# Small matmuls of a head pair in turns over the two row halves, outputs of four chunks by kind

## The chip, the cores and the metric

The kernel runs on one core of one Trainium2 chip. The metric is the device time of one execution in microseconds, less is better; the figure for a kernel is the median of its timed runs.

## The reference

One layer of a hybrid decoder on a sequence of 1024 tokens with 2048 channels, all in float32. The input is RMS-normalised and multiplied by one wide matrix; the columns go to four mixers and a gate. The mixers are RWKV-7 (8 heads of 64 channels, a state of 64x64 per head that is carried from token to token by a delta rule), windowed attention (window 128, 8 query heads over 2 key heads, with sinks and a linear position bias), causal pooling, and a spatial gating unit. Their outputs are multiplied by SiLU of the gate, go through an output projection, are normalised and added to the input:

```python
h = rms_norm(x, pre_w)
za, zb, zc, zd, gate = jnp.split(h @ w_in, SPLITS, axis=-1)
ya = rwkv7_mixer(token_shift(za, mu), ...)
yb = swa_sink_attention(zb, sinks)
yc = pool_mixer(zc, pool_w, pool_scale)
yd = spatial_gating(zd, sgu_norm_w, sgu_w, sgu_b)
y = jnp.concatenate([ya, yb, yc, yd], axis=-1) * jax.nn.silu(gate)
return x + rms_norm(y @ w_out, post_w)
```

## The kernel before

The sequence is taken in two halves of 512 tokens. Channels lie on the partitions. The input projection goes in tiles of 128 columns (`proj`, L260): for each of 16 tiles of the contraction there are three products of 128x128 by 128x512 (L273, L274, L275), because weights and input are split into a high and a low part; ScalarE makes the high part of the weights (L162) and VectorE the low part (L163). The output projection (L769 to L771) has the same form.

The mixers are generators. `mixers` (L866) emits one projection per turn and then lets each mixer take a small step (`yield` ends a step), so that a mixer's small instructions stand between projections. RWKV works on pairs of heads: channels 0 to 63 of a tile are one head, 64 to 127 the other, and `H[0]`, `H[1]` are these two halves of the partitions. A matmul that contracts over one half uses one row half of the PE array. Per pair and half sequence there are 8 chunks of 64 tokens.

The places that the change touches:

- `rwkv_prep`, L395 to L404: scores of each chunk, for `q` = 0 and 1 (four chunks each) and for each head. A head's four matmuls write one PSUM tile, and VectorE evicts it in three instructions (L402 to L404).
- `rwkv_prep`, L477 to L481: transposes of a head's 8 chunks into a PSUM tile, which ScalarE copies out.
- `rwkv_chain`, `outputs` (L504): after every fourth chunk (`YB`), the outputs of these four chunks are emitted. Each chunk has two matmuls over all 128 rows (L506) and two over 64 rows (L508), which add to the same part of the tile `yp`. The chain itself (L515, L523, L528) carries the state from chunk to chunk.
- `attention`, `scores` (L587): scores of a block of 128 queries, for the two row halves `x`, and two query heads `a` in each; L595, or L598 and L599 for the first block.

PSUM tiles come from small pools: `ps_pr` has two banks (RWKV preparation and other uses), `ps_ot` two (attention and others), `ps_y` and `ps_ch` one each. A tile can be written when what read its bank before is done. For the first scores of a pair (`q` = 0) the second `ps_pr` bank holds the sums of squares `pss` (L384) until VectorE has read them (L387). For the transposes the second bank holds the product of L469 until VectorE has copied it (L471).

The order in which the program is written isn't the order in an engine's queue. The framework lays the queues out when it builds the kernel: it takes instructions by priority (earlier in the program first, the weight loads and splits ahead of them) as they become ready by its own estimate of times, so later instructions can be put before earlier ones that still wait. At run time each engine's queue is worked off with semaphores. A float32 matmul stands in the trace as two records, a transpose and a product of the two projections as one.

Of the kernel before, what the change touches and what calls it, by code (L numbers as in the profile page):

```python
"""Hybrid decoder layer (RWKV-7, windowed attention, causal pooling, spatial gating) on one core.

The sequence is taken in two halves of 512 tokens. Activations are kept with channels on the
partitions. The operands of the two large projections are split into a high part that float32r holds
exactly and the exact remainder, and three products of the parts are added up in float32.
RWKV runs in chunks of 64 tokens: each chunk's delta rule is a triangular system, whose inverse is
built from 16x16 blocks by forward substitution and then merged; the state passes from chunk to chunk.
"""
# [15 lines left out]
PSUM = bass.MemoryType.PSUM  # L24
DRAM = bass.MemoryType.DRAM

P = 128
# [5 lines left out]
HD = 64  # L33
C = 64
NC = T // C
NHP = 4
WIN = 128
# [8 lines left out]
YB = 4  # L46
# [9 lines left out]
class Layer:  # L56
    def __init__(self, tc, es, A, out):
        self.tc, self.nc, self.A, self.out = tc, tc.nc, A, out
        self.n = 0
        self.ahead = {}  # L60

        def pool(name, bufs, **kw):
            return es.enter_context(tc.tile_pool(name=name, bufs=bufs, **kw))

        self.cp = pool("const", 1)
        self.gp = pool("gen", 78)
        self.wrp = pool("wraw", 3)
        self.whp = pool("whi", 3)
        self.wlp = pool("wlo", 3)
        self.sm = pool("small", 4)  # L70
        self.fp = pool("fsub", 1)
        self.dp = pool("scratch", 2, space=DRAM)
        self.dpc = pool("blocks", 1, space=DRAM)
        self.ps_pj = pool("ps_pj", 2, space=PSUM)
        self.ps_pr = pool("ps_pr", 2, space=PSUM)
        self.ps_ch = pool("ps_ch", 1, space=PSUM)
        self.ps_y = pool("ps_y", 1, space=PSUM)
        self.ps_ot = pool("ps_ot", 2, space=PSUM)
        # the first activation loads the engine's tables while the first data is under way
        warm = self.tile(self.sm, [P, 1], "warm")  # L80
        self.nc.vector.memset(warm, 0.0)
        self.nc.scalar.activation(out=warm, in_=warm, func=AF.Square)
        self.constants()
# [57 lines left out]

# [1 line left out]
    def rsqrt(self, x, n, scale, eps):  # L143
        """1 / sqrt(x * scale + eps) for a [128, n] tile, by Newton's iteration."""
        v_ = self.nc.vector
# [18 lines left out]

# [1 line left out]
    def x_load(self, hf, k):  # L166
# [4 lines left out]
    def x_square(self, k, x, accs):  # L171
        """Adds the squares of 128 channels of each token to one of the sums."""
        nc = self.nc
# [8 lines left out]
    def x_rstd(self, hf, accs):  # L182
        """1/rms of each token of the half, along the free dim of every partition."""
        nc = self.nc
# [13 lines left out]
    def first_half(self):  # L198
        """The first half's input, whose 1/rms is applied to its projections, and that 1/rms."""
        nc = self.nc  # L200
# [50 lines left out]

# [1 line left out]
    def w_load(self, m, half):  # L253
# [23 lines left out]

# [1 line left out]
    def gate(self, j, branch):  # L279
# [7 lines left out]

# [1 line left out]
    def shift(self, pz, m, out):  # L289
# [20 lines left out]
    def head_rows(self, d, h):  # L310
        """A head's 64x64 matrices, in DRAM, as [row, chunk, column]."""
        d = d[h * NC * CSTEP:(h + 1) * NC * CSTEP].rearrange("(c r) -> c r", r=CSTEP)[:, 0:C * C]
        return d.rearrange("c (s t) -> s c t", t=C)

    def diagonal(self, d):
        """The 16x16 diagonal blocks of both heads' matrices as [block, row, column]."""
        d = d.rearrange("(i r) -> i r", r=CSTEP // 4)[:, 0:16 * C]
        return d.rearrange("i (s t) -> i s t", t=C)[:, :, 0:16]

    def rwkv_prep(self, hp):  # L320
# [37 lines left out]
        yield  # L358
        # in-context keys and keys of each chunk, (b | k) for the first head and (k | b) for the second
        bk = []  # L360
        for q in range(2):
# [3 lines left out]
            for h in range(2):  # L365
                ob, ok = slice(C * h, C * h + C), slice(C * (1 - h), C * (2 - h))
                nc.vector.tensor_tensor(out=b[H[h], :, ob], in0=v3(g1[:, qs])[H[h]], in1=v3(fa[:, qs])[H[h]], op=ALU.mult)
                nc.vector.tensor_tensor(out=b[H[h], :, ok], in0=v3(g1[:, qs])[H[h]], in1=v3(f[:, qs])[H[h]], op=ALU.mult)
        # per head: its own channels hold (a | r) of each chunk, the other half the masked key scores
        comb = [[self.g([P, 4, 2 * C]) for q in range(2)] for h in range(2)]  # L370
# [8 lines left out]
        yield  # L379
        # 1 / max(|k k_k|^2, 1e-24) with tokens of a chunk on the partitions  # L380
        pss = self.ps(self.ps_pr)
# [13 lines left out]
        for q in range(2):  # L395
            yield
            cs = slice(q * 4, q * 4 + 4)
            for h in range(2):
                p, o = self.ps(self.ps_pr, [P, 4, P]), H[1 - h]
                for c in range(4):  # L400
                    nc.tensor.matmul(p[:, c], bk[q][H[h], c, :], comb[h][q][H[h], c, :], start=True, stop=True)  # L401
                nc.vector.tensor_tensor(out=L[H[h], cs], in0=p[H[h], :, 0:C], in1=mr[H[h], cs], op=ALU.mult)  # L402
                nc.vector.tensor_tensor(out=M[H[h], cs], in0=p[H[h], :, C:2 * C], in1=mki4[H[h]], op=ALU.mult)
                nc.vector.tensor_tensor(out=comb[h][q][o], in0=p[o], in1=mk4[o], op=ALU.mult)  # L404
        yield
        # inverses of the 16x16 diagonal blocks, a block on each partition
        LB = self.tile(self.fp, [64, 16, 16], "LB")
# [19 lines left out]
        for _ in range(DMA_STEPS):  # L427
            yield
        # merges to 32, then to 64
        L32 = self.g([P, NC, C])  # L430
        nc.gpsimd.tensor_tensor(out=L32, in0=L, in1=self.m32.unsqueeze(1).to_broadcast([P, NC, C]), op=ALU.mult)

        def part(t, i):
            """The columns of the first or second 16 of every 32."""
            return t.rearrange("p c (b i u) -> p c b i u", b=2, i=2)[:, :, :, i]
# [36 lines left out]
        yield  # L472
        # tokens on the partitions: (b; k) of each head, and v beside the state
        BK = [self.g([P, NC, HD]) for h in range(2)]
        SV = [self.g([P, NC, HD]) for h in range(2)]
        UV = [self.g([P, NC, HD]) for h in range(2)]
        for h in range(2):  # L477
            p = self.ps(self.ps_pr, [P, NC, HD])
            for c in range(NC):
                nc.tensor.transpose(p[:, c], bk[c // 4][H[h], c % 4, :], self.ident[H[h], H[h]])  # L480
            nc.scalar.copy(out=BK[h], in_=p)  # L481
        p = self.ps(self.ps_pr, [P, NC, HD])
# [14 lines left out]
    def rwkv_chain(self, st):  # L497
# [5 lines left out]

        def outputs(c):  # L504
            for h in range(2):
                nc.tensor.matmul(yp[H[h], c], comb[h][c // 4][:, c % 4, C:2 * C], SV[h][:, c], start=True, stop=False)  # L506
            for h in range(2):
                nc.tensor.matmul(yp[H[h], c], M[H[h], c], UV[h][H[h], c], start=False, stop=True)  # L508

        for c in range(NC):  # L510
# [25 lines left out]
            if c % YB == YB - 1:  # L536
                for i in range(c + 1 - YB, c + 1):
                    outputs(i)
        yield
# [23 lines left out]

# [1 line left out]
    def attention(self, hf):  # L565
# [21 lines left out]
        def scores(b, g, k0):  # L587
            sc = []
            for x in range(2):
                p = self.ps(self.ps_ot, [P, 2, 2 * WIN])  # L590
                s = self.g([P, 2, 2 * WIN])
                for a in range(2):
                    qb = q[2 * g + a][H[x], b * P:(b + 1) * P]
                    if b:
                        nc.tensor.matmul(p[:, a], qb, kd[g][H[x], (b - 1) * P:(b + 1) * P], start=True, stop=True)  # L595
                        continue
                    if hf:
                        nc.tensor.matmul(p[:, a, 0:WIN], qb, self.kprev[g][H[x]], start=True, stop=True)  # L598
                    nc.tensor.matmul(p[:, a, WIN:], qb, kd[g][H[x], 0:P], start=True, stop=True)  # L599
                for a in range(2):  # L600
# [63 lines left out]

# [1 line left out]
    def pooling(self, hf):  # L666
# [36 lines left out]

# [1 line left out]
    def gating_unit(self):  # L705
# [48 lines left out]

# [1 line left out]
    def out_weights(self, cb, i, hi, lo):  # L756
        """Two 128-row tiles of a 512-column block of w_out, split."""
        with self.tc.high_priority():
# [25 lines left out]
    def out_proj(self, hf, back=None):  # L784
# [28 lines left out]
        if not last:  # L813
            for _ in back:
                pass
            return ssq
        # the last column block, one token tile after the other
        w = []
# [47 lines left out]
    def mixers(self, hf, back, start):  # L866
        """Emits the projections, and between them the mixers' work in small steps."""
        self.y, self.y_split, fed = [None] * KT, [], 1
# [126 lines left out]
```

## Time and profile before

| | |
|---|---|
| median of 3 timed runs | 1835.55 us (1832.64 to 1838.29) |
| span of the profiled execution, first to last instruction | 1831.1 us |
| between span and median | 4.45 us |
| PE busy | 1783.8 us, 97% of the span |
| VectorE busy | 986.4 us, 54% |
| ScalarE busy | 615.8 us, 34% |
| GpSimd busy | 347.2 us, 19% |
| DMA | 190 MB, mean 104 GB/s |

The profiled execution's own time is its span and what lies around it (the start and end of the program, which hold no instruction). Busy means that at least one instruction of the engine was under way. The lines of the trace are read with their tiles: `ps_pr<-g,g` is a matmul into a tile of pool `ps_pr` from two tiles of pool `g`. In "64*128 64x128" the stationary operand has 64 rows and 128 columns, and the moving one 64 rows and 128 columns.

### The profile page before, as it was taken

How to read it: one execution, taken by the hardware profiler on the slowest of the kernel's cores; microseconds unless marked ns; L12 is line 12 of the kernel's file. 1: busy time of each engine (PE TensorE's matmuls, PEld its weight loads, DVE VectorE, ACT ScalarE, POOL GpSimd, SP SyncE). 2: the span in 40 equal slices, each digit the busy share in tenths (PEclk: the TensorE clock that was granted, in tenths of full speed). 3: DMA queues.
4: the chain of work that ended last, by engine and by line, in shares of the span. 5: the costliest groups of instructions: out<-in, count | busy, mean ns of one | idle time of the engine just before them, and what ended most of it. 6: DMA issues, size and time to landing. Idle time of an engine off the chain costs nothing.

```text
span 1831.1 us, 26853 instructions
## 1 busy us (share of the span) xinstructions
PE 1783.8 (97%) x10352; PEld 1359.3 (74%) x10352; DVE 986.4 (54%) x2186; ACT 615.8 (34%) x1205; POOL 347.2 (19%) x506
## 2 busy tenths in 40 slices
PE   7999999999999999999999999999999999999997
PEld 5787677667767877788877876677777678778875
DVE  6654676476456644753346446754753564353335
ACT  6323333433333322433232333333323323242230
POOL 4111231122134311110002223311220220100002
PEclk9999999999998999999999998999999899999999
DMA  6342113123223312454333532342232132224445
GB/s 205 101 120 76 59 54 96 58 70 103 93 86 94 119 58 70 144 168 129 130 114 105 164 105 80 110 142 76 70 102 76 52 98 73 71 77 123 146 134 201
DMA packets 58144, 190.00 MB, mean 104 GB/s; under 512 B 8400, under 2 KB 8400, under 8 KB 58016
## 3 DMA queue, kind: packets, MB, share of 16 engines
q1 hardware_dynamic: 44672, 147.34, 25.1%
q0 software_dynamic: 13200, 40.91, 7.6%
q8 instruction: 81, 1.33, 0.3%
q14 instruction: 47, 0.39, 0.1%
q10 hardware_dynamic: 144, 0.03, 0.0%
HBM read 168.86 MB, written 18.87 MB: 103 GB/s over the span
## 4 chain that ended last, share of the span: by engine, by line
PE 86%; DVE 7%; issue 3%; DMA 1%; ACT 1%; POOL 0%; DVEq 0%; SPq 0%; ACTq 0%; POOLq 0%
PE ps_pj L273 18%; PE ps_pj L274 17%; PE ps_pj L275 17%; PE ps_pj L769 3%; PE ps_pj L771 3%; PE ps_pj L770 3%; PE ps_pr L769 3%; PE ps_pr L771 3%; PE ps_pr L770 3%; PE ps_pr L401 2%; PE ps_y L508 1%; DVE wl L163 1%; PE ps_ot L643 1%; PE ps_pr L442 1%; PE ps_ch L523 1%
## 5 line engine op out<-in xcount | busy, mean ns | idle before, releaser
L163 DVE TENSOR_TENSOR wl<-wr,wh 128x512 fp32r<-128x512 f32 x488 | 346.9, 712 | 512.1 <-ACT wh L162 493.7
L273 PE MATMUL ps_pj<-g,wh 128*128 128x512 f32 x1472 | 603.6, 410 | 12.2 <-ACT g L212 12.2
L275 PE MATMUL ps_pj<-g,wl 128*128 128x512 f32 x1472 | 595.0, 404 | 5.4 <-DVE wl L163 5.2
L162 ACT CAST wh<-wr 128x512 fp32r<-128x512 f32 x488 | 301.7, 620 | 877.0 <-PE ps_pj L274 624.8
L274 PE MATMUL ps_pj<-g,wh 128*128 128x512 f32 x1472 | 594.9, 404 | 0.0
L273 PEld LDWEIGHTS ps_pj<-g,wh 128*128 128x128 f32 x1472 | 281.1, 191 | 84.7 <-ACT g L212 12.2
L275 PEld LDWEIGHTS ps_pj<-g,wl 128*128 128x128 f32 x1472 | 280.6, 191 | 74.1 <-DVE wl L163 7.1
L274 PEld LDWEIGHTS ps_pj<-g,wh 128*128 128x128 f32 x1472 | 280.6, 191 | 67.2 <-issue 4.9
L518 POOL TENSOR_SCALAR SD<-g,g 64x64 f32<-64x64 f32 x128 | 63.3, 494 | 523.2 <-DVE g L531 367.1
L769 PE MATMUL ps_pj<-wh,g 128*128 128x512 f32 x224 | 88.6, 396 | 0.4 <-DVE g L879 0.2
L769 PE MATMUL ps_pr<-wh,g 128*128 128x512 f32 x224 | 88.4, 395 | 0.0
L771 PE MATMUL ps_pr<-wh,g 128*128 128x512 f32 x224 | 88.3, 394 | 0.0
L770 PE MATMUL ps_pr<-wl,g 128*128 128x512 f32 x224 | 88.2, 394 | 0.0
L770 PE MATMUL ps_pj<-wl,g 128*128 128x512 f32 x224 | 88.1, 393 | 0.0
L771 PE MATMUL ps_pj<-wh,g 128*128 128x512 f32 x224 | 88.0, 394 | 0.0
L811 POOL DMA_DIRECT2D dram_o<-g x24 | 13.0, 541 | 246.5 <-DVE g L781 243.1
L531 DVE SCALAR_TENSOR_TENSOR g<-ps_ch,g,SD 64x64 f32<-64x64 f32 x112 | 31.7, 283 | 51.2 <-PE ps_ch L528 48.8
L879 DVE TENSOR_TENSOR g<-ps_pj,g 128x512 f32<-128x512 f32 x45 | 30.9, 687 | 46.8 <-PE ps_pj L275 46.1
L417 DVE TENSOR_TENSOR ftmp<-t,LB 64x1 f32<-64x1 f32 (+14 forms) x120 | 45.3, 377 | 14.7 <-DMA LB<-dl 11.4
L769 PEld LDWEIGHTS ps_pj<-wh,g 128*128 128x128 f32 x224 | 42.1, 188 | 10.9 <-DVE g L879 0.7
L769 PEld LDWEIGHTS ps_pr<-wh,g 128*128 128x128 f32 x224 | 42.1, 188 | 10.4 <-DVE g L781 0.7
L771 PEld LDWEIGHTS ps_pj<-wh,g 128*128 128x128 f32 x224 | 42.1, 188 | 10.0
(239 smaller groups left out, 2111.9 us busy)
## 6 DMA issues: line engine op xcount, KB each, us to landing
wr<-in_w_in SPq DMA_DIRECT2D x188, 512.0 KB, 3.7
wr<-in_w_out SPq DMA_DIRECT2D x64, 512.0 KB, 3.6
g<-in_xT POOLq DMA_DIRECT2D x32, 256.0 KB, 6.0
g<-in_x POOLq DMA_DIRECT2D x32, 256.0 KB, 4.7
out_y<-g SPq DMA_DIRECT2D x32, 256.0 KB, 3.9
dram_o<-g POOLq DMA_DIRECT2D x24, 256.0 KB, 3.5
g<-dram_o POOLq DMA_DIRECT2D x24, 256.0 KB, 4.1
g<-in_xT SPq DMA_DIRECT2D x16, 256.0 KB, 5.9
```

The source lines that it names most:

```text
L162: self.nc.scalar.copy(out=hi, in_=raw)
L163: self.nc.vector.tensor_tensor(out=lo, in0=raw, in1=hi.bitcast(F32), op=ALU.subtract)
L273: nc.tensor.matmul(p, hi[:, kk], hh, start=k == 0, stop=False)
L274: nc.tensor.matmul(p, hi[:, kk], hl, start=False, stop=False)
L275: nc.tensor.matmul(p, lo[:, kk], hh, start=False, stop=k == KT - 1)
L401: nc.tensor.matmul(p[:, c], bk[q][H[h], c, :], comb[h][q][H[h], c, :], start=True, stop=True)
L417: nc.vector.tensor_tensor(out=tmp[:, 0:i, 0:i], in0=T16[:, 0:i, 0:i].rearrange("p j c -> p c j"), in1=LB[:, 0:i, i].unsqueeze(1).to_broadc ...
L518: nc.gpsimd.tensor_scalar(out=SD[H[h]], in0=SV[h][H[h], c], scalar1=E[H[h], c, C:C + 1], scalar2=None, op0=ALU.mult)
L531: nc.vector.scalar_tensor_tensor(out=SV[h][H[h], c + 1], in0=pt[H[h], 2], scalar=E[H[h], c, C:C + 1], in1=SD[H[h]], op0=ALU.mult, op1=ALU.add)
L769: nc.tensor.matmul(p, yh[:, ms], hi, start=k == 0, stop=False)
L770: nc.tensor.matmul(p, yh[:, ms], lo, start=False, stop=False)
L771: nc.tensor.matmul(p, yl[:, ms], hi, start=False, stop=k == KT - 1)
```

## The change

In the scores of RWKV, the transposes and the attention scores, the PSUM tiles of both row halves are taken before the first matmul, and the matmuls alternate between the halves instead of finishing one half first. The evictions follow as before, half by half. In `outputs` the matmuls of four chunks are grouped by kind: first the eight over 128 rows, then the eight over 64 rows. Since all chunks share one PSUM bank, only the first chunk now carries the `start` flag. No instruction is added or taken away. Comments and docstrings are blanked (not shown).

```diff
-            for h in range(2):
-                p, o = self.ps(self.ps_pr, [P, 4, P]), H[1 - h]
-                for c in range(4):
-                    nc.tensor.matmul(p[:, c], bk[q][H[h], c, :], comb[h][q][H[h], c, :], start=True, stop=True)
+            pq = [self.ps(self.ps_pr, [P, 4, P]) for h in range(2)]
+            for c in range(4):
+                for h in range(2):
+                    nc.tensor.matmul(pq[h][:, c], bk[q][H[h], c, :], comb[h][q][H[h], c, :], start=True, stop=True)
+            for h in range(2):
+                p, o = pq[h], H[1 - h]
...
+        pb = [self.ps(self.ps_pr, [P, NC, HD]) for h in range(2)]
+        for c in range(NC):
+            for h in range(2):
+                nc.tensor.transpose(pb[h][:, c], bk[c // 4][H[h], c % 4, :], self.ident[H[h], H[h]])
         for h in range(2):
-            p = self.ps(self.ps_pr, [P, NC, HD])
-            for c in range(NC):
-                nc.tensor.transpose(p[:, c], bk[c // 4][H[h], c % 4, :], self.ident[H[h], H[h]])
-            nc.scalar.copy(out=BK[h], in_=p)
+            nc.scalar.copy(out=BK[h], in_=pb[h])
...
-        def outputs(c):
-            for h in range(2):
-                nc.tensor.matmul(yp[H[h], c], comb[h][c // 4][:, c % 4, C:2 * C], SV[h][:, c], start=True, stop=False)
-            for h in range(2):
-                nc.tensor.matmul(yp[H[h], c], M[H[h], c], UV[h][H[h], c], start=False, stop=True)
+        def outputs(cs):
+            for c in cs:
+                for h in range(2):
+                    nc.tensor.matmul(yp[H[h], c], comb[h][c // 4][:, c % 4, C:2 * C], SV[h][:, c], start=c == 0,
+                                     stop=False, skip_group_check=True)
+            for c in cs:
+                for h in range(2):
+                    nc.tensor.matmul(yp[H[h], c], M[H[h], c], UV[h][H[h], c], start=False, stop=c == NC - 1,
+                                     skip_group_check=True)
...
             if c % YB == YB - 1:
-                for i in range(c + 1 - YB, c + 1):
-                    outputs(i)
+                outputs(range(c + 1 - YB, c + 1))
...
-            for x in range(2):
-                p = self.ps(self.ps_ot, [P, 2, 2 * WIN])
-                s = self.g([P, 2, 2 * WIN])
-                for a in range(2):
+            px = [self.ps(self.ps_ot, [P, 2, 2 * WIN]) for x in range(2)]
+            for a in range(2):
+                if b == 0 and hf:
+                    for x in range(2):
+                        nc.tensor.matmul(px[x][:, a, 0:WIN], q[2 * g + a][H[x], 0:P], self.kprev[g][H[x]], start=True, stop=True)
+                for x in range(2):
                     qb = q[2 * g + a][H[x], b * P:(b + 1) * P]
                     if b:
-                        nc.tensor.matmul(p[:, a], qb, kd[g][H[x], (b - 1) * P:(b + 1) * P], start=True, stop=True)
-                        continue
-                    if hf:
-                        nc.tensor.matmul(p[:, a, 0:WIN], qb, self.kprev[g][H[x]], start=True, stop=True)
-                    nc.tensor.matmul(p[:, a, WIN:], qb, kd[g][H[x], 0:P], start=True, stop=True)
+                        nc.tensor.matmul(px[x][:, a], qb, kd[g][H[x], (b - 1) * P:(b + 1) * P], start=True, stop=True)
+                    else:
+                        nc.tensor.matmul(px[x][:, a, WIN:], qb, kd[g][H[x], 0:P], start=True, stop=True)
+            for x in range(2):
+                p = px[x]
+                s = self.g([P, 2, 2 * WIN])
```

## Rows read from the trace of the kernel before

**Rows 1.** Page, part 4: chain that ended last, shares by engine.

```profile
PE 86%; DVE 7%; issue 3%; DMA 1%; ACT 1%; POOL 0%; DVEq 0%; SPq 0%; ACTq 0%; POOLq 0%
```

**Rows 2.** Groups by line on PE: busy us, mean ns of one, idle before.

```profile
L401 PE MATMUL ps_pr<-g,g 64*128 64x128 f32 x256 | 39.1, 320 | 4.3 <-DVE g L374 4.3
...
L508 PE MATMUL ps_y<-g,g 64*64 64x64 f32 x256 | 32.7, 249 | 0.0
...
L506 PE MATMUL ps_y<-g,g 128*64 128x64 f32 x256 | 26.8, 241 | 0.0
...
L595 PE MATMUL ps_ot<-g,g 64*128 64x256 f32 x96 | 20.8, 423 | 0.0
...
L480 PE MATMUL ps_pr<-shapes,g 64*128 64x64 f32 x128 | 11.8, 234 | 0.0
```

**Rows 3.** Timeline of PE, 79 to 85 us: start, length, line, count.

```profile
79.82 1.13 PE L401 MATMUL ps_pr<-g,g 64*128 64x128 f32 x8 [1.51 <-DVE g L374]
...
82.16 0.40 PE L275 MATMUL ps_pj<-g,wl 128*128 128x512 f32 x1
82.50 1.14 PE L401 MATMUL ps_pr<-g,g 64*128 64x128 f32 x8
...
84.13 0.39 PE L275 MATMUL ps_pj<-g,wl 128*128 128x512 f32 x1
84.36 0.40 PE L273 MATMUL ps_pj<-g,wh 128*128 128x512 f32 x1
```

**Rows 4.** Timeline of PE, 93 to 96 us.

```profile
93.45 1.71 PE L401 MATMUL ps_pr<-g,g 64*128 64x128 f32 x16
```

**Rows 5.** Timeline, first, second and last pass: eviction L387 and the first head's run.

```profile
82.20 0.16 DVE L387 TENSOR_SCALAR r<-ps_pr 128x8 f32<-128x8 f32 x1
...
227.47 1.16 PE L401 MATMUL ps_pr<-g,g 64*128 64x128 f32 x8
227.58 0.17 DVE L387 TENSOR_SCALAR r<-ps_pr 128x8 f32<-128x8 f32 x1 [0.36 <-PE ps_pr L384]
...
1454.45 1.82 PE L401 MATMUL ps_pr<-g,g 64*128 64x128 f32 x8 [0.63 <-DVE g L374]
...
1456.57 0.16 DVE L387 TENSOR_SCALAR r<-ps_pr 128x8 f32<-128x8 f32 x1
```

**Rows 6.** Timeline of PE, 186 to 189 us: outputs of a half head pair.

```profile
186.62 0.34 PE L515 MATMUL ps_ch<-g,g 128*64 128x64 f32 x4
...
187.00 0.33 PE L508 MATMUL ps_y<-g,g 64*64 64x64 f32 x4
187.26 0.34 PE L506 MATMUL ps_y<-g,g 128*64 128x64 f32 x4
187.53 0.33 PE L508 MATMUL ps_y<-g,g 64*64 64x64 f32 x4
...
188.06 0.66 PE L635 MATMUL ps_ot<-shapes,g 128*128 128x128 f32 x4
```

**Rows 7.** Timeline of PE: half of one score call, and a whole one.

```profile
252.69 1.13 PE L595 MATMUL ps_ot<-g,g 64*128 64x256 f32 x4
...
279.08 1.14 PE L595 MATMUL ps_ot<-g,g 64*128 64x256 f32 x8
```

**Rows 8.** Timeline, 159 to 161 us: first transposes, and evictions L471.

```profile
159.94 0.71 PE L480 MATMUL ps_pr<-shapes,g 64*128 64x64 f32 x8
160.05 0.85 DVE L471 COPY g<-ps_pr 32x256 f32<-32x256 f32 x2 [0.51 <-PE ps_pr L469]
```

**Rows 9.** Timeline of PE, 205 us: two row halves, two banks.

```profile
205.09 0.69 PE L330 MATMUL ps_pr<-g,g 64*128 64x512 f32 x1
205.10 0.69 PE L332 MATMUL ps_pr<-g,g 64*128 64x512 f32 x1
```

**Rows 10.** Spans and clocks: granted TensorE clock, mean.

```profile
core 0: 1831.1 us, clock 0.977
```

## The prediction

> **What bounds the kernel now.** I read the chain that ended last first, because it says whose time counts: PE holds 86% of it [rows 1], so a microsecond of PE time is worth about one microsecond of the end. Then the groups by line on PE. The lines that the change touches are busy for 39.1 (L401), 32.7 (L508), 26.8 (L506), 20.8 (L595) and 11.8 us (L480) [rows 2], 131 us together; more than a part of that can't be had. The timelines show how long a run of such records really takes, and what stands between two runs. The reader is to see there how much two row halves already run side by side.
>
> **What the change does to the queue.** The number of matmuls, DMAs and evictions stays the same, and so does the number of banks. Only PE's order moves, and no other queue, SP's and POOL's included, gets or loses an instruction. So each part is a question: do the records of two row halves overlap more than today?
>
> **What a run costs today.** A head's four score matmuls (eight records) take 1.13 to 1.14 us [rows 3]. Seen in the stream of projections: from the product at 82.16 to the one at 84.13 there are 1.97 us with three products and the run; a product takes 0.23 (84.13 to 84.36), so the run costs 1.97 - 0.69 = 1.28 us [rows 3].
>
> **How far the halves overlap today.** Matmuls of two row halves into two banks can start 0.01 us apart [rows 9]. And they do so without being written in turns: a run of 16 score records, first head then second, takes 1.71 us, not twice 1.13 [rows 4]; eight records of attention scores, first four of one half and then four of the other, take 1.14 us, as long as four records alone (1.13) [rows 7]. So PE looks ahead about four records: with runs of four per half the overlap is whole, with runs of eight it is half.
>
> The Trainium skill ("TensorE: Matmul & The Clock Gate", Part 3, the mechanism) says that only weight loads are pulled ahead and that matmuls are strictly first in, first out. By that rule a run that is written half by half would be serial today, and each of the 16 RWKV score groups and 12 attention calls would halve, which is the rival of full pairing below. The rows disagree: 1.71 us for 16 and 1.14 for 8 [rows 4, 7].
>
> **RWKV scores, second four chunks (`q` = 1).** Here the 16 records stand together [rows 4]; there are eight such groups (four head pairs, two halves). Written in turns they overlap whole and take as long as eight alone: 1.71 - 1.14 = 0.57 us less, 8 times: 4.5 us. Between 0 (the look-ahead doesn't change) and 4.5 I take 4.5, since in attention runs of four, and so surely runs of two, overlap whole [rows 7].
>
> **RWKV scores, first four chunks (`q` = 0).** Here the heads' runs stand apart, the first at 79.82, the second at 82.50 with projections between [rows 3]. The reason is the second bank: VectorE evicts `pss` from it at 82.20 [rows 5], and only then can the second head write. The change doesn't free that bank sooner, and the planner takes what is ready: the first head's four matmuls will go ahead as now. Upper bound: both runs in one, 1.28 us less, 8 times: 10.2 us. Lower bound: 0. I take 2.0, one microsecond for each of the two of the eight groups in which L387 falls inside the first head's run, as at 227.58 in the run from 227.47 [rows 5].
>
> **Transposes.** The first head's eight take 0.71 us from 159.94 and are done at 160.65; the second bank is evicted by L471 from 160.05 to 160.90 [rows 8]. The second head comes too late to overlap, in turns or not. Between 0 and 0.71 x 8 = 5.7 us I take 0.
>
> **Attention scores.** A call that stands together overlaps whole already [rows 7]. Others are broken up by the RWKV chain's instructions or by a bank that isn't free, and stay so. Upper bound: the 12 calls of L595 at 1.14 us each [rows 7] take 13.7 of today's 20.8 us [rows 2]: 7.1. I take 1.0.
>
> **Outputs.** After L515 of a chunk the planner puts the outputs that are ready: L506, L508, L506, L508, L506, four records each, 1.44 us from 186.62 to 188.06, L515's records included [rows 6]; there are 16 such stretches, two per pair and half. Each change between 128 rows and 64 costs: L515 with L506, eight records of one shape, take 0.38 (186.62 to 187.00), four of L506 between two changes 0.27 (187.26 to 187.53). So four more records cost 0.11, and the change 0.16. Grouped by kind there are 16 records of 128 rows (0.16 + 4 x 0.11 = 0.60) and 8 of 64 rows (0.26 from 187.00 to 187.26, and 0.11: 0.37): 0.97 instead of 1.44, 0.47 less, 16 times: 7.5 us. Lower bound 0, if L506 of the last chunk, which waits for the chain's state, were to hold back the group; I don't take it, since in the rows the planner puts ahead what is ready. The evictions of `yp` come a step later, so a projection covers an output that is put back.
>
> **Evictions.** The first head's eviction now waits for the last but one matmul of both. Paired, that is again about 1.1 us after the start [rows 3]: nothing. If the second head is late, at most the first's eviction comes that much later, and the projection that stands between two steps (48 products of 0.23 us, 11 us) covers it.
>
> **Sum.** 4.5 + 2.0 + 0 + 1.0 + 7.5 = 15.0 us. The profiled span of 1831.1 becomes 1816.1; the timed median lies 4.45 us above the span, so 1835.55 becomes **1820.5 us**.
>
> **Rivals.**
>
> *Full pairing.* If the planner, given the turns, waits for both banks with other work in between and then issues both heads together, every part gets its upper bound: 10.2 + 4.5 + 5.7 + 7.1 + 7.5 = 35.0 us, 1800.5 us. For it: projections are always there to fill in. Against it: the first head's matmuls are ready earlier and are now taken as soon as they are [rows 3]. The skill's rule on strict order would give this number too.
>
> *The second bank holds up the queue.* If the second head's first matmul stands second in PE's queue, all behind it waits: the other three matmuls of the first head, and the projections after them, until L387: 2.54 us at first (79.82 to 82.36), 0.28 at 227.47, 2.28 at last (1454.45 to 1456.73) [rows 3, 5], 15.6 us over the eight; and for the transposes until L471, 0.96 us (159.94 to 160.90) [rows 8] 8 times, 7.7. Less the gains that the pairing then brings (10.2 + 4.5 + 5.7 + 7.5 = 27.9) that leaves 4.6 us: 1831 us. The Trainium skill ("TensorEngine Tiling (Array Packing)", Restrictions and Gotchas, PSUM pressure) names this price: row tiles need banks of their own. A cousin is that the gain goes into waits on VectorE (L401 waits 4.3 us for it already [rows 2]): 1835.5. Both are no change by the measure here.
>
> *The clock.* The mean granted clock is 0.977 [rows 10]; with the two levels 2.4 and 1.2 GHz that is 4.6% of the span, 84 us, at the lower one, which costs 42 us. The last pass shows one: eight records take 1.82 us instead of 1.13, after PE had waited 0.63 us for VectorE [rows 3, 5]. These stages have small matmuls and waits. If the denser runs leave more waiting and the time at the lower level grows by 30 us, the gain is gone; from 41 us on the kernel is slower by over 0.3%; if it doubles, it is 42 - 15 = 27 us slower, 1862 us. For it: the fall lies where the change works. Against it: the same work in less time with projections moving up should rather raise PE's activity.
>
> **How the numbers follow.** The forecast 0.47 (1812 to 1828), full pairing 0.15, held queue or lost gain 0.23, the clock 0.15. Differences within 0.3%, 5.5 us, can't be told from no change. Faster: 0.47 + 0.15 = 0.62; same 0.23; slower 0.15. The range reaches from 1797 (just past full pairing) to 1840 (lost gain, and the first of the clock): it leaves out nearly all of the clock's 0.15 and a little of full pairing, under 2 in 10. The forecast's own range is 1812 to 1828: half of the sum, or the sum with the first scores (5.1 for 2.0), the transposes (2.8 for 0) and attention (3.5 for 1.0) at half their upper bounds.
>
> **What would show it.** After the change the 16-record runs of L401 last about 1.14 us, not 1.71, at all eight places of `q` = 1; for `q` = 0 two runs of eight still stand apart. After L515 there is a run of 12 L506 and one of 8 L508 records, about 0.97 us in all. L480 still stands in two runs of eight, L595's calls take 1.14 us as before. Full pairing shows as 16 L480 records in under 0.9 us. The held queue shows as idle time of PE in front of L401 and L480, released by L387 and L471. The clock shows in the mean granted clock, under 0.977. Wrong would be: runs of 16 that still take 1.7 us, or shape changes that cost nothing in the new order.

## The result, and the profile after

The changed kernel takes 1805.23 us (median of 4 runs, 1799.19 to 1812.52) against 1835.74 us for the kernel before, a ratio of 0.984 with a 95% interval of 0.9807 to 0.9872: 30.5 us less, where 15.0 were predicted, so twice the forecast. The time lies inside the range and below the 1812 to 1828 of the forecast itself.

The views of after in the order of those of before. The spans and clocks, which answer to [rows 10]:

```profile
core 0: 1806.3 us, clock 0.981
```

The chain that ended last, shares by engine, which answers to [rows 1]:

```profile
PE 83%; DVE 9%; issue 3%; DMA 3%; ACT 1%; POOL 1%; DVEq 0%; SPq 0%; POOLq 0%; ACTq 0%
```

PE is still the bound. The profiled span is 24.8 us shorter, and part of that is the clock. What the lower clock level costs a span, reckoned as the prediction did, is the span times what the mean clock lacks to one: 1831.1 x 0.023 = 42.1 us before, 1806.3 x 0.019 = 34.3 after. So 7.8 of the 24.8 us are clock, and 17.0 are work and waits. The time of every execution on record is 1.7 to 1.9 us above its own span (1808.09 and 1806.3 in the profiled one). The 4.45 us between span and median before were therefore mostly spread between executions, and the 30.5 us of the medians hold some of that spread too.

The groups by line, which answer to [rows 2] (L515 was L508, L511 was L506, L604 was L595, L482 was L480):

```profile
L401 PE MATMUL ps_pr<-g,g 64*128 64x128 f32 x256 | 32.6, 315 | 5.9 <-DVE g L374 5.9
L515 PE MATMUL ps_y<-g,g 64*64 64x64 f32 x256 | 22.0, 239 | 0.0
L604 PE MATMUL ps_ot<-g,g 64*128 64x256 f32 x96 | 20.7, 420 | 0.0
L511 PE MATMUL ps_y<-g,g 128*64 128x64 f32 x256 | 19.1, 229 | 0.1
L482 PE MATMUL ps_pr<-shapes,g 64*128 64x64 f32 x128 | 11.8, 234 | 0.0
```

The two lines of the outputs fell from 59.5 to 41.1 us busy, the scores from 39.1 to 32.6. Attention and transposes stand where they stood. The reader is to see here where to look first: the largest fall is in the outputs, not in the scores.

PE's timeline in four places: the first scores (`q` = 0) from 79 us, the second scores (`q` = 1) from 97, the transposes from 163, and one attention call at 308:

```profile
79.36 2.05 PE L401 MATMUL ps_pr<-g,g 64*128 64x128 f32 x8 [1.53 <-DVE g L374]
...
97.10 0.40 PE L275 MATMUL ps_pj<-g,wl 128*128 128x512 f32 x1
97.42 1.16 PE L401 MATMUL ps_pr<-g,g 64*128 64x128 f32 x16
98.51 0.50 PE L273 MATMUL ps_pj<-g,wh 128*128 128x512 f32 x1
...
163.40 0.71 PE L482 MATMUL ps_pr<-shapes,g 64*128 64x64 f32 x8
...
164.93 0.71 PE L482 MATMUL ps_pr<-shapes,g 64*128 64x64 f32 x8
...
308.38 1.14 PE L604 MATMUL ps_ot<-g,g 64*128 64x256 f32 x8
```

Sixteen score records last 1.16 us, where they lasted 1.71 [rows 4], as predicted. At `q` = 0 the first head's eight records go alone, as before; at one of the eight places only (1118.86 us) the heads stand together. The transposes are two runs of eight, and a whole attention call takes 1.14 us as it did [rows 7].

The outputs of one half of a head pair, which answer to [rows 6]:

```profile
190.07 0.34 PE L523 MATMUL ps_ch<-g,g 128*64 128x64 f32 x4
190.23 0.52 PE L511 MATMUL ps_y<-g,g 128*64 128x64 f32 x12
190.69 0.66 PE L645 MATMUL ps_ot<-shapes,g 128*128 128x128 f32 x4
...
194.39 0.33 PE L511 MATMUL ps_y<-g,g 128*64 128x64 f32 x2
...
195.25 0.28 PE L511 MATMUL ps_y<-g,g 128*64 128x64 f32 x2
195.46 0.50 PE L515 MATMUL ps_y<-g,g 64*64 64x64 f32 x9
...
196.78 0.33 PE L515 MATMUL ps_y<-g,g 64*64 64x64 f32 x2
```

This isn't what was predicted. The twelve records over 128 rows stand where they were expected, and with the four of L523 they take 0.62 us to the next instruction (predicted 0.60). But the eight over 64 rows don't follow. They come only behind the last chunk's four of L511, at 195.46, 4.8 us after the place where they were expected (190.69), and then mostly in one run.

### The profile page after: what moved, and what is told of

The parts are those of the page before. It is cut to its first block, busy times and chain, and to the rows that moved or that the text cites. A ratio compares the mean times of both kernels' runs of the same rounds, so it can differ in the third digit from the quotient of the medians.

```text
span 1806.3 us, 26854 instructions
## 1 busy us (share of the span) xinstructions
PE 1754.0 (97%) x10352; PEld 1344.7 (74%) x10352; DVE 988.4 (55%) x2186; ACT 614.9 (34%) x1205; POOL 347.8 (19%) x506
## 4 chain that ended last, share of the span: by engine, by line
PE 83%; DVE 9%; issue 3%; DMA 3%; ACT 1%; POOL 1%; DVEq 0%; SPq 0%; POOLq 0%; ACTq 0%
PE ps_pj L273 18%; PE ps_pj L274 17%; PE ps_pj L275 17%; PE ps_pj L779 3%; PE ps_pj L781 3%; PE ps_pj L780 3%; PE ps_pr L780 3%; PE ps_pr L781 3%; PE ps_pr L779 3%; DVE wl L163 1%; PE ps_pr L401 1%; PE ps_pr L444 1%; DVE ftmp L419 1%; PE ps_y L515 1%; PE ps_ot L653 1%
## 5 line engine op out<-in xcount | busy, mean ns | idle before, releaser
L779 PEld LDWEIGHTS ps_pr<-wh,g 128*128 128x128 f32 x224 | 42.2, 188 | 10.6 <-DVE g L791 0.8
L781 PEld LDWEIGHTS ps_pj<-wh,g 128*128 128x128 f32 x224 | 42.1, 188 | 9.8
```

Of the source, the lines that this page charges most:

```text
L779: nc.tensor.matmul(p, yh[:, ms], hi, start=k == 0, stop=False)
L781: nc.tensor.matmul(p, yl[:, ms], hi, start=False, stop=k == KT - 1)
```

## The experiments

Two measures stand in what follows. The **ratio** is to the kernel before, with its 95% interval. The **clock-free difference** is a kernel's mean span times its mean granted clock over all its runs, less the same for the kernel before (1833.4 x 0.9770 = 1791.2, 59 runs). It takes out what the prediction's reckoning gives to the clock. The other kernels have 4 to 12 runs, `runs4` one. A **run** of outputs is an unbroken series of matmuls of one of the two output lines, in the order in which PE starts them (one of a matmul's two records is counted). A **change of rows** is a place where two records that PE starts one behind the other contract over different numbers of rows (128, 64 or 32) and at least one of them is an output; it is counted over all records.

| kernel | median us | ratio | mean clock | clock-free difference, us |
|---|---|---|---|---|
| changed | 1805.23 | 0.984 (0.9807 to 0.9872) | 0.9835 | -17.2 |
| changed, timed again | 1808.81 | 0.9848 (0.9811 to 0.9885) | 0.9818 | -18.0 |
| `outputs_only` | 1811.24 | 0.9854 (0.983 to 0.9879) | 0.9812 | -16.5 |
| `scores_only` | 1836.68 | 1.0007 (0.9985 to 1.0028) | 0.9765 | 0.0 |
| `bk_att_only` | 1832.83 | 0.9971 (0.9953 to 0.9989) | 0.9775 | -1.1 |
| `three_one` | 1828.29 | 0.9967 (0.9944 to 0.9989) | 0.9786 | -3.9 |
| `late` | 1821.85 | 0.9918 (0.9886 to 0.995) | 0.9743 | -19.6 |
| `late_both` | 1816.92 | 0.9895 (0.9861 to 0.9929) | 0.9803 | -12.5 |
| `step_late` | 1801.22 | 0.9811 (0.9782 to 0.984) | 0.9804 | -26.9 |
| `all_late` | 1794.04 | 0.9775 (0.9747 to 0.9803) | 0.9815 | -31.3 |
| `all_late_plain` | 1799.56 | 0.9811 (0.9784 to 0.9837) | 0.9796 | -29.3 |
| `runs4` | 1808.81 (one run) | | 0.981 | -18.5 |

### Each part alone

Each is the kernel before with hunks of the change as they are printed in its diff above. `outputs_only` has `outputs` and its call:

```diff
-        def outputs(c):
+        def outputs(cs):
...
-                for i in range(c + 1 - YB, c + 1):
-                    outputs(i)
+                outputs(range(c + 1 - YB, c + 1))
```

`scores_only` has the turns of the RWKV scores:

```diff
+            pq = [self.ps(self.ps_pr, [P, 4, P]) for h in range(2)]
+            for c in range(4):
+                for h in range(2):
+                    nc.tensor.matmul(pq[h][:, c], bk[q][H[h], c, :], comb[h][q][H[h], c, :], start=True, stop=True)
...
```

`bk_att_only` has the turns of the transposes and of attention:

```diff
+        pb = [self.ps(self.ps_pr, [P, NC, HD]) for h in range(2)]
...
+            px = [self.ps(self.ps_ot, [P, 2, 2 * WIN]) for x in range(2)]
...
```

The changed kernel was timed again beside `three_one`, `late` and `late_both`.

> The kernel before with the outputs of four chunks grouped by kind, and nothing else changed. Theory 1 (PE's records): most of the gain is here; the two lines of the outputs take about 16 us less from start to next start, as in the changed kernel, so 1835.7 becomes about 1820, with three runs per half head pair (12 and 4 records over 128 rows, then 12 over 64 rows) where there were eleven. Theory 2 (the clock): about 12 us of the measured 30 come from fewer stretches at the lower clock, and not from these lines; then this part alone gives 16 us only if the mean granted clock stays near 0.977, and up to 25 us if it rises to 0.985.

> The kernel before with the RWKV scores alone written in turns. Theory 1: eight runs of 16 records take 1.09 us in place of 1.64 to the next start, 4.5 us less; the first four chunks still stand in two runs of eight and give nothing: about 1831. Theory 2: the clock moves by itself with any new order, so the time may lie anywhere within 10 us of 1831 and the granted clock tells where. Rival: if the second bank held up the queue, PE would idle in front of the scores and the time would be 1835 or more.

> The kernel before with the transposes and the attention scores written in turns. Theory 1: nothing moves that counts: the transposes still stand in two runs of eight of 0.64 us, whole attention calls still take 1.07 us to the next start: 1835 plus or minus 3. Theory 2: if the lower clock is set off by chance by any change of order, this kernel too leaves 1835 by more than 5 us with a clock other than 0.977.

> The changed kernel once more, for the spread of its granted clock: 1800 to 1813 us, and about 1809 us of span when brought to a mean clock of 0.98 with the slope of 16 us per 0.01 that the runs so far show. If the gain were mostly a matter of the clock, the clock would fall back to 0.976 in some of these runs and the time to 1820.

The outputs alone bring nearly the whole gain (-16.5 of about -17.5), transposes and attention together -1.1, the scores nothing where about 1831 us was expected. Yet the scores' run is shorter in `scores_only` too. PE's timeline there, in two places:

```profile
97.29 1.16 PE L401 MATMUL ps_pr<-g,g 64*128 64x128 f32 x16
...
1172.82 0.39 PE L274 MATMUL ps_pj<-g,wh 128*128 128x512 f32 x1
1174.78 0.66 PE L637 MATMUL ps_ot<-shapes,g 128*128 128x128 f32 x4 [1.56 <-ACT g L678]
```

and PE's waits by line there: total, times, longest (L401 has its 4.2 us as before, 4.3):

```profile
PE ps_ot L676 <- DVE g L604: 3.0, 3, 1.8
...
PE ps_ot L637 <- ACT g L678: 2.1, 2, 1.6
```

The same transposes in the kernel before, PE's waits:

```profile
PE ps_ot L635 <- ACT g L676: 0.4, 1, 0.4
```

Laid side by side record by record, the profiles of before and of `scores_only` differ by 4.1 us at the scores, all of it gained. Attention gives back 1.4, other small stages 2.4, the stretches with equal instructions 1.3, and stretches at the lower clock in either profile gain 0.7; the first product starts 0.9 us earlier. The spans lie 0.7 us apart (1830.4 and 1831.1). So the term was there in PE's records and not in the end. Waits for other engines explain a part of that: without the first wait of the kernel, PE is idle for 36.9 us where it was idle for 35.1, and the wait of L637 for ScalarE alone is 1.7 us longer, most of it at 1174.78. Where the other 2.3 us of the 4.1 went isn't shown: each of these places may pay for the scores, or for the planner's new order as such.

### Why the outputs brought twice the term

Theory: the matmuls that write one PSUM tile are kept in written order. All eight chunks share one tile, so behind `wide` of the fourth chunk, which waits for the chain's state, the 64-row ones of the first three are held too, and the runs become longer than predicted. `three_one` writes down the order that the prediction had assumed; everything else is as in the change.

```diff
+            def wide(cc):
+                for c in cc:
+                    for h in range(2):
+                        nc.tensor.matmul(yp[H[h], c], comb[h][c // 4][:, c % 4, C:2 * C], SV[h][:, c], start=c == 0,
+                                         stop=False, skip_group_check=True)
+
+            def half(cc):
+                for c in cc:
+                    for h in range(2):
+                        nc.tensor.matmul(yp[H[h], c], M[H[h], c], UV[h][H[h], c], start=False, stop=c == NC - 1,
+                                         skip_group_check=True)
+
+            wide(cs[0:3])
+            half(cs[0:3])
+            wide(cs[3:4])
+            half(cs[3:4])
```

> The changed kernel with the outputs in the order that the prediction expected: over 128 rows for the first three chunks, over 64 rows for these three, then both kinds for the fourth. Theory 1 (writes to one bank stay in the written order, so that the changed kernel holds the 64-row outputs back behind the fourth chunk's and so makes runs of 12 of them): this order splits them again, 8 and four times 2 records; it gives up half of the outputs' gain, 8 us slower than the changed kernel at the same clock, about 1817 of span at 0.98. Rival (only the changes of shape in the stretch behind the third chunk count): 0.97 us in that stretch as predicted, and the same time as the changed kernel.

PE's timeline in `three_one` (L531 is the chain's, L512 over 128 rows, L518 over 64):

```profile
185.57 0.34 PE L531 MATMUL ps_ch<-g,g 128*64 128x64 f32 x4
185.74 0.52 PE L512 MATMUL ps_y<-g,g 128*64 128x64 f32 x12
186.19 0.45 PE L518 MATMUL ps_y<-g,g 64*64 64x64 f32 x8
186.57 0.66 PE L653 MATMUL ps_ot<-shapes,g 128*128 128x128 f32 x4
```

Here is the predicted stretch to the letter: 12 and 8 records, 1.00 us from 185.57 to 186.57, predicted 0.97. And the kernel gains 3.9 us clock-free, not 17: at the same clock it is about 14 us slower than the changed kernel, where 8 were expected. So the stretch was priced well, and its order was the wrong one: it is the held order that brings the rest. Only the written order differs between the two kernels, so the hold by written order is shown. Nor did all of the stretch's price reach the end. PE is busy for 1770.6 of 1826.5 us here and for 1783.8 of 1831.1 before, so its idle time went from 47.3 to 55.9 us. The largest rise is at the chain, before (first) and in `three_one`:

```profile
PE ps_ch L523 <- DVE X L521: 3.4, 8, 1.4
...
PE ps_ch L539 <- DVE X L537: 6.7, 10, 1.9
```

If long runs are what counts, the outputs should be held longer still. `step_late` issues each four chunks one step later, when the fourth's state is ready; `all_late` issues all eight behind the whole chain.

```diff
         for c in range(NC):
             yield
+            if c == 4:
+                outputs(range(4))
...
-            if c % YB == YB - 1:
-                outputs(range(c + 1 - YB, c + 1))
         yield
+        outputs(range(4, NC))
```

In `all_late` the first two added lines are left out, and the last is `outputs(range(NC))`.

> The changed kernel with the outputs of four chunks emitted one step later, when the fourth chunk's state is there: 16 and 16 records in one go, 32 runs in PE's queue in place of 110. Theory 1: 78 runs fewer, up to 20 us less than the changed kernel at the same clock, 1789 of span at 0.98, and all_late no more than 5 us better than this. Rival as for all_late: 1806 or more.

> The changed kernel with the outputs of all eight chunks emitted a step after the chain, 32 records over 128 rows and then 32 over 64 rows at eight places: 16 runs in PE's queue where the changed kernel has 110 and the kernel before 180. Theory 1 (what is paid is each separate run, with a change of shape into it and out of it, about 0.26 us by the 18 us that 70 fewer runs gave): 94 runs fewer, up to 24 us less than the changed kernel at the same clock, 1785 of span at 0.98; half of it, 12 us, if the chain's steps miss the outputs as filling. Rival (the outputs were useful filling while the chain waits for VectorE): PE idles in the chain instead, and the time is 1806 or more.

PE's timeline in `step_late`:

```profile
203.44 0.69 PE L511 MATMUL ps_y<-g,g 128*64 128x64 f32 x16
204.05 0.68 PE L515 MATMUL ps_y<-g,g 64*64 64x64 f32 x16
204.66 0.34 PE L525 MATMUL ps_ch<-g,g 128*64 128x64 f32 x4
```

PE's timeline in `all_late`:

```profile
243.91 1.15 PE L511 MATMUL ps_y<-g,g 128*64 128x64 f32 x32
245.00 1.15 PE L515 MATMUL ps_y<-g,g 64*64 64x64 f32 x32
246.07 1.16 PE L401 MATMUL ps_pr<-g,g 64*128 64x128 f32 x16
```

Sixteen records of one kind hold PE for 0.61 us, thirty-two for 1.09. The second sixteen thus cost 0.48, 0.03 a record, and 0.13 us is left as the price of each change of shape; the prediction had 0.16 and 0.11 for four records from [rows 6]. The outputs' time on PE goes with the number of changes. "To the next start" is the sum over the outputs' records of the time until PE starts its next record, with time at the lower clock counted half:

| kernel | runs of outputs | changes of rows | busy us, both lines | to the next start, us | PE idle, us |
|---|---|---|---|---|---|
| before | 180 | 206 | 59.5 | 45.2 | 47.3 |
| `three_one` | 132 | 162 | 48.9 | 38.4 | 55.9 |
| changed | 110 | 112 | 41.1 | 30.5 | 52.3 |
| `step_late` | 32 | 26 | 21.9 | 19.6 | 56.6 |
| `all_late` | 16 | 10 | 18.4 | 17.3 | 53.3 |

In busy time that is between 0.22 and 0.26 us for each run fewer than before (10.6 / 48, 18.4 / 70, 37.6 / 148, 41.1 / 164). To the next start it is between 0.14 and 0.16 us for each change of rows fewer (6.8 / 44, 14.7 / 94, 25.6 / 180, 27.9 / 196), near the price of 0.13 read off two single stretches. In clock-free time a run fewer is worth 0.25, 0.18 and 0.19 us in the last three kernels and 0.08 in `three_one`; the end doesn't follow PE's records one for one, since changed overlaps and waits elsewhere count in it too. Number and place of the runs move together in these kernels, so the end's gain isn't split between fewer changes and a later place; PE's own time to the next start is what the count explains.

The expectations had up to 20 us less than the changed kernel at the same clock for `step_late`, and for `all_late` up to 24, or 12 if the chain misses the filling; about 9 and 14 came. `all_late` is the fastest kernel of the study, 1794.04 us.

Does it need the turns? `all_late_plain` is the kernel before with `all_late`'s outputs and no turns anywhere.

```diff
-            if c % YB == YB - 1:
-                for i in range(c + 1 - YB, c + 1):
-                    outputs(i)
         yield
+        outputs(range(NC))
```

> The kernel before with all_late's outputs and nothing of the turns: scores, transposes and attention as before the change. Theory 1 (the turns shorten eight runs of scores by 0.55 us, but attention then waits for VectorE by about as much): within 2 us of all_late at the same clock, 1795 to 1798 of span at 0.98. Rival (the turns' 4.4 us come through once the outputs no longer fill the waits): 4 us or more slower than all_late, 1800 or more.

It gives -29.3 against -31.3: all three sets of turns together are worth about 2.0 us there, and 0.7 to 1.5 between `outputs_only` and the changed kernel. The medians lie 5.5 us apart, but their intervals of the ratio overlap, and much of the 5.5 is the clock (0.9796 and 0.9815).

### What the turns do to PE

`runs4` writes the scores in turns of two matmuls (four records) for each head instead of one.

```diff
-            for c in range(4):
+            for c0 in (0, 2):
                 for h in range(2):
-                    nc.tensor.matmul(pq[h][:, c], bk[q][H[h], c, :], comb[h][q][H[h], c, :], start=True, stop=True)
+                    for c in (c0, c0 + 1):
+                        nc.tensor.matmul(pq[h][:, c], bk[q][H[h], c, :], comb[h][q][H[h], c, :], start=True, stop=True)
```

> The changed kernel with the RWKV scores in turns of two matmuls (four records) per head in place of one. Theory 1 (PE starts a matmul of the other row half past four waiting records): the 16 records of the second four chunks take as long as in strict turns, 1.09 us to the next start, at all eight places where they stand together. Rival (matmuls start strictly in the order of the queue): the second of each pair of runs waits for the first, 1.6 us or more.

PE's timeline in `runs4`:

```profile
97.10 1.26 PE L402 MATMUL ps_pr<-g,g 64*128 64x128 f32 x16
98.29 0.50 PE L273 MATMUL ps_pj<-g,wh 128*128 128x512 f32 x1
```

From start to next start the sixteen take 1.19 us, in strict turns 1.09 (97.42 to 98.51 above). Half by half they last 0.55 us longer than in turns (1.71 against 1.16). So runs of four overlap nearly whole and runs of eight only in part, as the prediction read from [rows 4, 7]. The starts of the single records say the same. In strict turns the sixteen start as eight pairs, at most 0.01 us apart. Half by half, in the kernel before, four start alone first, and three pairs in all are found; in fours there are seven pairs, the first of them at once. A record of the second head thus starts past three or four waiting ones of the first, and "by half" was a little too much for runs of eight. The queue itself isn't in the trace: that it held the records as written, and that PE did the pairing and not the planner, is taken for granted here. The Trainium skill ("TensorE: Matmul & The Clock Gate", Part 3) keeps matmuls in program order and lets only weight loads go ahead; by that rule the second head would start behind all eight records of the first, and eights would last nearly two times 1.13 us. The rows show 1.71, and in fours 1.26.

### Giving the second bank time

The changed kernel's first scores wait 1.53 us for VectorE and then last 2.05 us for eight records (above), where a run at the full clock lasts 1.13 [rows 3]; the granted clock is 0.50 there, 1.2 GHz:

```profile
79.40:84.20 4.80, 4.80 (x15) 3.54 (x15) 3.52 (x10) 0.63 (x1) 1.04 (x1) 0.50 0.27 94
```

The wait alone can't be the reason, since the kernel before waits as long at the same place (1.51 us [rows 3]) and has a granted clock of 1.00 from 77 to 83 us. Theory: without that wait there is no fall of the clock there, and the heads pair up as well. `late` issues the scores of `q` = 0 two steps later; `late_both` also the transposes (the last two added lines).

```diff
         for q in range(2):
             yield
+            if q == 0:
+                yield
+                yield
...
+        yield
+        yield
         BK = [self.g([P, NC, HD]) for h in range(2)]
```

> The changed kernel with the first four chunks' scores two steps later, behind the next projection. Theory 1 (the second bank, held by the sums of squares until VectorE has read them, keeps the heads apart): now both banks are free, the 16 records stand together at all eight places and take 1.09 us, so 1.28 us less each, 10 us in all, and PE no longer waits for VectorE in front of them, so that the stretches at the lower clock there (about 35 us in the changed kernel) go too, up to 17 us more: 1778 to 1797. Rival: the preparation ends a projection later and the chain's end is exposed where no projection is left: 1805 or more.

> As the last, and the transposes two steps later too. Theory 1: the 16 transposes stand together and take half the time, about 0.7 us less at eight places, 5 us under the last: 1773 to 1792. Rival: the transposes are bound by the loads of their stationary operand and pair worse (16 in 1.0 us or more), or the later chain costs what they give: the same as the last or slower.

PE's timeline and waits in `late`:

```profile
89.12 1.16 PE L404 MATMUL ps_pr<-g,g 64*128 64x128 f32 x16
90.22 0.50 PE L273 MATMUL ps_pj<-g,wh 128*128 128x512 f32 x1
```

```profile
PE ps_ot L687 <- DVE g L615: 13.2, 2, 8.4
```

PE's timeline, and its waits, in `late_both`:

```profile
178.19 0.71 PE L487 MATMUL ps_pr<-shapes,g 64*128 64x64 f32 x16
```

```profile
PE ps_pr L570 <- POOL g L563: 14.9, 4, 7.1
...
PE ps_ot L689 <- DVE g L617: 10.3, 4, 4.5
```

The pairs came in part. In `late` the wait is gone, and of the eight groups of `q` = 0 two stand as unbroken sixteens; in the other six both heads' records stand close together, but cut by other instructions. In `late_both` four of all sixteen groups are unbroken, and at all eight places sixteen transposes last 0.71 us, as long as eight. The time didn't follow (expected were 1778 to 1797 and 1773 to 1792 us). `late` is at -19.6 (the changed kernel -17.2 and -18.0), with a mean clock of 0.9743: in its profile PE is at the lower clock for 87 us, where the changed kernel has 71, for the most part at other places, so the theory that the falls vanish falls. PE waits 13.2 us at L687 for VectorE, where after had 3.0 at the same place. `late_both` is at -12.5: the lines behind the transposes come later, and PE waits for POOL 14.9 us at L570, 1.4 in the kernel before and after.

Not tried: both heads' scores in one bank.

## Why the prediction was right or wrong, point by point

- **Scores, `q` = 1 (-4.5).** The mechanism and its size are right in the records: 0.55 us at each place where the sixteen stood unbroken before. Those are six of the eight, not all; attention's records cut the other two. Over all scores PE's time falls by 4.1 us in `scores_only`. In the time it isn't there (`scores_only`, 0.0). The step that failed is the first sentence of all, that a microsecond of PE's time is worth about one of the end: 1.8 us of it are more waiting, most of it for ScalarE, and the rest stays open. With long runs of outputs part of it seems to stay (2.0 us for all the turns).
- **Scores, `q` = 0 (-2.0).** One group of eight paired, not two. Right in kind; what it is worth in the time isn't shown by itself.
- **Transposes (0) and attention (-1.0).** The runs are unchanged, as predicted, and the two edits alone give -1.1. That this is attention's 1.0 isn't shown: in the changed kernel attention's records take as long to the next start as before (27.0 and 26.8 us).
- **Outputs (-7.5).** The direction and the price of a change of shape are right, the size is off by more than two: 16.5 measured. The step that failed is "in the rows the planner puts ahead what is ready". The lower bound had named the case in which the last chunk holds back the group, as a loss. It happened, and was a gain: held records come in longer runs. The sum also priced one stretch of five runs, where a half head pair has about eleven (180 / 16), and left the others as they were. Where exactly the predicted order was written (`three_one`), PE's time in the outputs fell by 6.8 us, near the 7.5, but only 3.9 came out at the end.
- **Sum (-15.0).** 17.0 clock-free in the profiles: nearly the forecast, because the outputs' surplus stands against the scores' missing gain. That is luck: the two largest terms are each wrong at the end, in opposite directions.
- **The clock.** The prediction took the clock as it was, and as a rival only for the worse, with the remark that less waiting should rather help. It helped: 0.977 to 0.981 in the profiles, 7.8 us, and 0.9770 to 0.9835 in the mean of the runs, which is 1810 x 0.0065 = 12 us; timed again, the changed kernel had 0.9818, 9 us. That brings the time below the forecast's own range. Of the single parts only the outputs carry it (0.9812 in `outputs_only`, 0.9765 and 0.9775 in the two others), and not in every kernel that has them (0.9743 in `late`). Why a longer run of outputs leaves less time at the lower level isn't settled.
- **Rivals.** Full pairing didn't happen, though its 1800.5 us is close to the result; in `late_both`, where all transposes paired and the scores did in pieces, the later steps cost more than the pairs gave; pairing without the delay wasn't tried. The held queue didn't either: L401 waits 5.9 us, not 15.6. But its cousin, the gain that goes into waits, happened to a part of the scores' term.

## What to carry to other kernels

Count the changes of matmul shape in PE's queue, above all between numbers of rows: small matmuls into one tile took least time here in one run for each shape, and holding them until all of their inputs are there can be worth more than issuing each as soon as it is ready (1794 against 1805 us here). Turns over the row halves shorten a run that is longer than PE's look-ahead, but test whether the time saved on PE reaches the end, because here it was gone at the end, in part into waits for other engines. Where a kernel's span is part clock, compare spans at equal clock before you give a difference to an edit.

## What the runs showed that was not expected

- Sixteen small matmul records in a row hold PE for 0.61 us and thirty-two for 1.09, 0.03 us a record, with 128 rows as with 64; a change between the two shapes costs 0.13 us there, and 0.14 to 0.16 over whole kernels. Of the 45.2 us of the outputs before, 512 records at 0.03 are 15 us, so the two kinds in four-record runs paid more for changes than for work.
- PE starts matmuls of the second row half past three or four waiting records of the first, if its queue holds them as written: 1.16 us for sixteen in turns, 1.26 in fours, 1.71 in eights.
- Over all these kernels, spans fall by 16.9 us for 0.01 more of the mean granted clock (one line for all of them, each with its own height), near the 18 us that the reckoning with span times clock gives.
- Waits that were taken away (`late`) didn't take the falls of the clock with them: the clock's mean went down, 0.9818 to 0.9743, while the clock-free time stayed.
